# The keys' low part on all 128 rows: the second score product of the causal attentions

## The chip, the cores and the metric

The kernel runs on one core of one Trainium2 chip. The metric is the time of one execution in device microseconds (us). The times below are medians of several executions; the trace is of one further execution, taken with the hardware profiler.

## The reference, cut to what matters

The program is two transformer blocks, one after the other, on 512 tokens of width 1024. The change lies in the first block, which has two layers. Each layer has a mixer with two kinds of attention, both with heads of width 64, and then a feed-forward part:

```python
# fox: 8 heads, causal, with a forget gate
s = jnp.einsum('bhqd,bhkd->bhqk', qi, k) * scale
s = s + ci[..., :, None] - c[..., None, :]
s = jnp.where(kpos[None, :] <= qpos[:, None], s, -jnp.inf)
p = jax.nn.softmax(s, axis=-1)
o = jnp.einsum('bhqk,bhkd->bhqd', p, v)
# nsa: 8 query heads in 2 groups that share keys and values; three branches
#   compressed keys (31 blocks), selected blocks, and a window of 512
o_n = g[..., 0:1] * o_c + g[..., 1:2] * o_s + g[..., 2:3] * o_w
```

With 512 tokens there are 8 blocks to select from and up to 16 may be taken, and the window is as long as the sequence, so the kernel computes the selected and the window branch as plain causal attentions, each with its own keys and values. Counted over a layer that makes 8 causal heads in fox and 16 in nsa (8 query heads, 2 branches); over both layers 16 and 32.

## The kernel before, in words

The matrix engine (PE) reads its operands as fp32r, a shorter format than fp32. To keep precision, the kernel splits a value into a high part (rounded to fp32r) and a low part (the rest), and adds up the products. A projection (`mm3`, lines 234 to 236) takes three matmuls for each 128 input features: high by high, high by low, low by high.

For scores the split is stacked on the rows, over which PE contracts. A head has 64 features. `q_stack` (from line 569) makes a tile `Q[h]` of 128 rows for each head: the 64 rows `own` (0 to 63 for an even head, 64 to 127 for an odd one) hold the query's high part, the other 64 rows its low part. `fox` makes the keys: `KH[:, h]` holds the key's high part on both halves of the rows (ScalarE copies, lines 467 and 468), and `KL` its low part on the head's own 64 rows alone (VectorE, line 469). `causal_scores` (from line 593) then computes, for each of the four blocks of 128 queries against the n = 128, 256, 384 or 512 keys up to its end:

- line 605: all 128 rows of `Q` by all of `KH`, which gives (query high + query low) by key high;
- line 606: the own 64 rows of `Q` by the own 64 rows of the low part, which gives query high by key low;
- in fox only, line 480: a constant selector of 128 rows by `cneg`, the forget gate's term;
- line 609: an identity by the causal mask in bf16, on the last 128 columns.

All four add up in one bank of PSUM. Then VectorE takes the row maximum (line 610), ScalarE the exponential with its sum (line 612), VectorE scales the rows (line 288), PE transposes the probabilities in pieces of 128x128 (line 629), VectorE and ScalarE copy them out into tiles `PT` (lines 635 and 633; tag `PT`, 4 buffers, used in pairs, one for each of two heads), and PE multiplies them by the values (line 638).

In `nsa` the keys of a branch lie in one tile `nK` with high and low part, and the low part is already written to both halves of the rows; yet line 606 reads only the own 64 of them. `nsa` rotates keys and queries with `rope_in` (from line 558): a shuffle (line 564), a multiply on GpSimd (line 565), a multiply and an addition on VectorE (lines 566 and 567). Its two scratch tiles `rsh` and `rzc` have one buffer each.

Within a mixer the instructions are written down in program order, but a list scheduler of the framework puts them in order for each engine, by its own estimate of their times, so that the products of attention and the projections of the parts that follow (`kp`, `vp`, `qp`, `mg`, `my` in the profile) are interleaved on PE. Buffers of one tag are handed on as they come free. In the odd mixer and the expert part of the second block the order on PE is written out by hand; the change does not touch them. All engines work through their own queue in order.

Of the kernel before, what the change touches and what calls it, by code (L numbers as in the profile page):

```python
# [11 lines left out]
F32 = mybir.dt.float32  # L12
F32R = mybir.dt.float32r
# [6 lines left out]
T = 512  # L20
# [127 lines left out]
class K:  # L148
# [303 lines left out]
    def fox(self, l, at, pp, w, XH, XL, v, cneg, B, comp):  # L452
        nc, C = self.nc, self.C
        ws, parts = {}, {}

        def project(pr):
            if pr % 2 == 0:
                ws[0] = [self.wcols(w, c + 128 * pr) for c in (0, 512)]
            wq, wk = [x[:, :, (pr % 2) * 128:(pr % 2) * 128 + 128] for x in ws[0]]
            Q = self.q_stack(at, pp, wq, XH, XL, None)  # L460
            zk = self.k_proj(at, pp, wk, XH, XL)
            KH = at.tile([128, 2, T], F32R, name="KH", bufs=2)
            KL = at.tile([128, T], F32R, name="KL", bufs=2)
            for h in range(2):
                own = slice(64 * h, 64 * h + 64)
                oth = slice(64 - 64 * h, 128 - 64 * h)
                nc.scalar.copy(KH[own, h], zk[own])
                nc.scalar.copy(KH[oth, h], zk[own])
                nc.vector.tensor_sub(KL[own], zk[own], KH[own, h])
            parts[pr] = Q, KH, KL  # L470

        def attend(pr):
            Q, KH, KL = parts.pop(pr)
            o = pp.tile([128, T], F32, name="o", tag="o")
            P, cf = [], []
            for h in range(2):
                own = slice(64 * h, 64 * h + 64)
                sel = C["sel"][:, 2 * pr + h:2 * pr + h + 1].to_broadcast([128, 128])

                extra = lambda s_, n: nc.tensor.matmul(s_[:, :n], sel, cneg[:, :n], start=False, stop=False)  # L480
                P.append(self.causal_scores(at, pp, Q[h], KH[:, h], Q[h][own], KL[own], extra))
                rs = at.tile([128, 4], F32, name="rs")
                nc.vector.reciprocal(rs, P[h][1])
                cf.append(rs)
            self.causal_pv(at, pp, o, P, cf,
                           [[v[:, k, (2 * pr + h) * 64:(2 * pr + h) * 64 + 64] for k in range(4)]
                            for h in range(2)], True, True)
            if pr:
                B.renew(pr)
            self.put_split(B, pr, o)  # L490

        project(0)
        next(comp)
        project(1)
        next(comp)
        for pr in range(4):
            attend(pr)
            if pr < 2:
                project(pr + 2)
# [58 lines left out]
    def rope_in(self, at, rc, rs, z):  # L558

        nc = self.nc  # L560
        n, c = z.shape
        sh = at.tile([128, T], F32, name="rsh", tag="rsh", bufs=1)[:n, :c]
        zc = at.tile([128, T], F32, name="rzc", tag="rzc", bufs=1)[:n, :c]
        nc.vector.stream_shuffle(sh, z, [i ^ 8 if i < 16 else i for i in range(32)])
        nc.gpsimd.tensor_mul(zc, z, rc)
        nc.vector.tensor_mul(sh, sh, rs)
        nc.vector.tensor_add(z, zc, sh)
# [22 lines left out]
        self.nc.vector.tensor_mul(z, ps, self.rB)  # L590
        return z

    def causal_scores(self, at, pp, Q, KH, qh, kl, extra=None):

        nc, C = self.nc, self.C
        P = at.tile([128, 1280], F32, name="P", bufs=3)
        sums = at.tile([128, 4], F32, name="sums", bufs=4)
        mx = at.tile([128, 4], F32, name="mx", bufs=4)
        views = []
        off = 0  # L600
        for i in range(4):
            n = 128 * (i + 1)
            qs = slice(128 * i, n)
            s = pp.tile([128, T], F32, name="s", tag="s")
            nc.tensor.matmul(s[:, :n], Q[:, qs], KH[:, :n], start=True, stop=False)
            nc.tensor.matmul(s[:, :n], qh[:, qs], kl[:, :n], start=False, stop=False)
            if extra is not None:
                extra(s, n)
            nc.tensor.matmul(s[:, qs], C["identb"], C["causal"], start=False, stop=True)  # L609
            nc.vector.tensor_reduce(mx[:, i:i + 1], s[:, :n], axis=X, op=OP.max, negate=True)  # L610
            pv = P[:, off:off + n]
            nc.scalar.activation(pv, s[:, :n], AF.Exp, bias=mx[:, i:i + 1], accum_out=sums[:, i:i + 1])  # L612
            views.append(pv)
            off += n
        return views, sums
# [25 lines left out]
    def nsa(self, l, p, at, pp, w, XH, XL, gate, gcmp, B, KC, VC, fill):  # L641
        nc, tc, I, C, rB = self.nc, self.tc, self.ins, self.C, self.rB
# [31 lines left out]
        for g in range(2):  # L674
            own = slice(64 * g, 64 * g + 64)
            Q = []
# [4 lines left out]
            s = pp.tile([128, 4, 4, 32], F32, name="s", tag="s")  # L681
            mask = C["cmpmask"].rearrange("p (t n) -> p t n", t=4)[:, :, None, :].to_broadcast([128, 4, 4, 32])
            nc.tensor.matmul(s, C["identb"], mask, start=True, stop=False)
            for t in range(4):
                qs = slice(128 * t, 128 * t + 128)
# [3 lines left out]
            s16 = s.rearrange("p t h n -> p (t h) n")  # L689
            mx = at.tile([128, 16], F32, name="cmx")  # L690
            nc.vector.tensor_reduce(mx, s16, axis=X, op=OP.max)
            Pc = at.tile([128, T], F32, name="Pc", tag="KL", bufs=2).rearrange("p (a n) -> p a n", n=32)
            nc.vector.tensor_sub(Pc, s16, mx[:, :, None].to_broadcast([128, 16, 32]))
            nc.scalar.activation(Pc, Pc, AF.Exp)
            cs = at.tile([128, 16], F32, name="cs")
# [19 lines left out]
            for s_ in range(2):  # L715
                kk = at.tile([128, 2, T], F32R, name="nK", tag="KH", bufs=2)
                kh, kl = kk[:, 0], kk[:, 1]
                for half in range(2):
                    o_ = slice(64 * half, 64 * half + 64)
                    nc.scalar.copy(kh[o_], zs[s_][own])  # L720
                for half in range(2):
                    o_ = slice(64 * half, 64 * half + 64)
                    nc.vector.tensor_sub(kl[o_], zs[s_][own], kh[own])
                for pr in range(2):
                    P, cf = [], []
                    for h in range(2):
                        hs = slice(64 * h, 64 * h + 64)
                        P.append(self.causal_scores(at, pp, Q[2 * pr + h], kh, Q[2 * pr + h][hs], kl[hs]))
                        rs = at.tile([128, 4], F32, name="rs")
                        nc.vector.reciprocal(rs, P[h][1])  # L730
                        hd = 4 * g + 2 * pr + h
                        nc.vector.tensor_mul(rs, rs, gate[:, :, 3 * hd + 1 + s_])
                        cf.append(rs)
                    self.causal_pv(at, pp, os_[pr], P, cf,
                                   [[vv[s_][:, k, 64 * g:64 * g + 64] for k in range(4)] for _ in range(2)],
                                   False, s_ == 1)
                    next(fill)
                    if pr:
                        next(fill)
# [4 lines left out]
    def compress(self, l, p, at, pp, w, XH, XL, B, mixed):  # L744
# [77 lines left out]
        KH = p.tile([128, 2, 32], F32R, name="KCH")  # L822
        KL = p.tile([128, 2, 32], F32R, name="KCL")
        zc3 = zc.rearrange("p (g n) -> p g n", g=2)
# [1222 lines left out]
```

## Time and profile before

| | |
|---|---|
| time, median of 3 runs | 3457.11 us (3451.3 to 3459.18) |
| profiled execution: its own time, its span | 3446.95 us, 3445.2 us |
| PE matmuls | busy 3255.6 us (94%), 14746 instructions |
| PE weight loads | busy 2111.6 us (61%) |
| VectorE (DVE) | busy 1553.8 us (45%) |
| ScalarE (ACT) | busy 1051.8 us (31%) |
| GpSimd (POOL) | busy 581.3 us (17%) |
| mean granted clock of PE | 0.978 |

The span runs from the first to the last instruction of the profiled execution. A busy share is an average over stages with different limits; matmuls are pipelined, so the durations of neighbours overlap, and what a matmul costs is read from one start to the next.

### The profile page before, as it was taken

To read this page: it belongs to the slowest core of one execution; us is meant where nothing else is said; L and a number is where in the kernel's file an instruction comes from. 1 tells how busy PE (TensorE), PEld (TensorE's weight loads), DVE (VectorE), ACT (ScalarE), POOL (GpSimd) and SP (SyncE) were. 2 spreads that over 40 slices of the span, in tenths; PEclk is the share of its full clock that TensorE was granted. 3 is DMA by queue.
4 is the path that set the end of the run, shared out by engine and by line. 5 is a ranking of instruction groups with operands and counts; after the bars stand their busy time and mean duration, and the time that the engine had idled before them with its cause. 6 is when DMAs were issued, how large, how long until landed. Compare 5 with 4: busy or idle time off the path is not lost. (4 is left out here: it accounts for less than half of the span.)

```text
span 3445.2 us, 37016 instructions
## 1 busy us (share of the span) xinstructions
PE 3255.6 (94%) x14746; PEld 2111.6 (61%) x14746; DVE 1553.8 (45%) x2435; ACT 1051.8 (31%) x1856; POOL 581.3 (17%) x437
## 2 busy tenths in 40 slices
PE   8999999999999999999998889999998889999997
PEld 5666678888766666888875676434345547444343
DVE  6555464334655545444458755122124666211214
ACT  3333333223344333322246423111113443111011
POOL 2012121001101111200121224000002552200001
PEclk9999999999999999999999989999999999999998
DMA  5101132224310111233321115999994113999997
GB/s 186 50 25 50 49 99 86 94 92 136 98 49 25 49 49 63 96 98 98 98 71 39 50 60 205 421 421 396 420 421 178 37 38 122 372 421 395 421 421 296
DMA packets 223724, 585.07 MB, mean 170 GB/s; under 512 B 17600, under 2 KB 160320, under 8 KB 173376
## 3 DMA queue, kind: packets, MB, share of 16 engines
q1 hardware_dynamic: 223120, 581.92, 44.6%
q8 instruction: 116, 1.90, 0.2%
q10 hardware_dynamic: 432, 0.79, 0.1%
q14 instruction: 56, 0.46, 0.0%
HBM read 580.57 MB, written 2.10 MB: 169 GB/s over the span
## 5 line engine op out<-in xcount | busy, mean ns | idle before, releaser
L225 ACT CAST whi<-w 128x1024 fp32r<-128x1024 f32 (+1 forms) x312 | 311.1, 1003 | 709.7 <-PE mm L235 501.6
L1725 PE MATMUL a<-w,xg 128*64 128x512 f32 x2048 | 477.6, 596 | 50.4 <-DMA w<-in_w_dram 50.4
L234 PE MATMUL mm<-h,whi 128*128 128x512 f32 x1056 | 416.3, 394 | 4.8 <-ACT whi L225 4.1
L236 PE MATMUL mm<-h,wlo 128*128 128x512 f32 x1056 | 414.3, 393 | 0.4 <-POOL wlo L228 0.3
L235 PE MATMUL mm<-l,whi 128*128 128x512 f32 x1056 | 412.2, 391 | 0.0
L228 DVE TENSOR_TENSOR wlo<-w,whi 128x1024 fp32r<-128x1024 f32 (+1 forms) x235 | 301.6, 1286 | 213.5 <-ACT whi L225 212.8
L1725 PEld LDWEIGHTS a<-w,xg 128*64 128x64 f32 x2048 | 155.1, 137 | 356.2 <-issue 249.5
L228 POOL TENSOR_TENSOR wlo<-w,whi 128x1024 fp32r<-128x1024 f32 x77 | 171.8, 2235 | 565.2 <-ACT whi L225 541.0
L234 PEld LDWEIGHTS mm<-h,whi 128*128 128x128 f32 x1056 | 198.7, 188 | 48.8 <-ACT whi L225 5.3
L236 PEld LDWEIGHTS mm<-h,wlo 128*128 128x128 f32 x1056 | 198.7, 188 | 45.7 <-DVE wlo L228 0.8
L235 PEld LDWEIGHTS mm<-l,whi 128*128 128x128 f32 x1056 | 198.7, 188 | 44.8 <-issue 0.7
L1725 PE MATMUL y<-w,hT 128*64 128x512 f32 x1024 | 224.7, 594 | 0.0
L1818 DVE SCALAR_TENSOR_TENSOR th<-th,a 128x512 f32<-128x512 f32 x32 | 22.0, 687 | 327.6 <-ACT th L1817 327.6
L610 DVE TENSOR_REDUCE mx<-s 128x1 f32<-128x128 f32 x192 | 93.4, 489 | 153.6 <-PE s L609 152.8
L1725 PEld LDWEIGHTS y<-w,hT 128*64 128x64 f32 x1024 | 72.0, 137 | 140.2 <-issue 138.1
L956 POOL TENSOR_TENSOR u<-u 128x512 f32<-128x512 f32 x64 | 66.6, 1040 | 521.4 <-ACT E L955 275.5
L612 ACT ACTIVATE P<-s,mx 128x128 f32<-128x128 f32 x192 | 101.1, 528 | 166.3 <-DVE mx L610 153.7
L1793 POOL TENSOR_TENSOR og<-OH,aff 128x512 f32<-128x512 f32 x16 | 16.8, 1048 | 716.5 <-DVE oT L1836 700.0
L1817 ACT ACTIVATE th<-a 128x512 f32<-128x512 f32 x32 | 19.1, 597 | 341.6 <-PE a L1725 341.6
L1857 DVE SCALAR_TENSOR_TENSOR yl<-y,gate,yh 128x512 fp32r<-128x512 f32 x32 | 24.0, 751 | 208.9 <-ACT yh L1856 208.9
L967 DVE TENSOR_TENSOR y<-mm,r 128x512 f32<-128x512 f32 x64 | 44.2, 691 | 160.7 <-PE mm L236 160.7
L629 PEld LDWEIGHTS pt<-c_ident,P 128*128 128x128 f32 x480 | 54.4, 143 | 76.1 <-issue 64.8
(614 smaller groups left out, 6326.5 us busy)
## 6 DMA issues: line engine op xcount, KB each, us to landing
w<-in_w_dram SPq DMA_DIRECT2D x384, 1024.0 KB, 12.9
w<-in_w_in_dram SPq DMA_DIRECT2D x32, 1024.0 KB, 5.2
w<-in_w_up_dram SPq DMA_DIRECT2D x32, 1024.0 KB, 5.4
w<-in_w_down_dram SPq DMA_DIRECT2D x32, 1024.0 KB, 5.1
w<-in_w_out_dram SPq DMA_DIRECT2D x8, 1024.0 KB, 5.1
w<-in_w_o_dram SPq DMA_DIRECT2D x8, 1024.0 KB, 4.7
w<-in_ple_gate_w_dram SPq DMA_DIRECT2D x16, 512.0 KB, 9.4
w<-in_w_in_even_dram SPq DMA_DIRECT2D x7, 1024.0 KB, 5.6
```

Of the source, the lines that this page charges most:

```text
L225: nc.scalar.copy(h, view)
L228: e.tensor_sub(l, view, h)
L234: mm(ps, wh, xh, start=first, stop=False)
L235: mm(ps, wh, xl, start=False, stop=False)
L236: mm(ps, wl, xh, start=False, stop=last)
L610: nc.vector.tensor_reduce(mx[:, i:i + 1], s[:, :n], axis=X, op=OP.max, negate=True)
L612: nc.scalar.activation(pv, s[:, :n], AF.Exp, bias=mx[:, i:i + 1], accum_out=sums[:, i:i + 1])
L629: nc.tensor.transpose(ps[:, (i - k) * 128:(i - k + 1) * 128], P[h][0][i][:, k * 128:(k + 1) * 128], C["ident"])
L956: nc.gpsimd.tensor_mul(u, u, u)
L967: nc.vector.tensor_mul(y, ps, r2)
L1725: nc.tensor.matmul(ps[64 * a:64 * a + 64], lhs(a, 4 * kc + k), cw[a][:, k], start=kc == 0 and k == 0, stop=kc == 1 and k == 3)
L1857: nc.vector.scalar_tensor_tensor(yl, y, gate, yh, op0=OP.mult, op1=OP.subtract)
```

## The change

The low part of the keys in fox becomes as wide as the high part, and line 606 takes all 128 rows in both attentions, with the same weights `Q[:, qs]` as line 605. So the product of the query's low part and the key's low part is now added as well. The two scratch tiles of `rope_in` give up their own buffers and take theirs from the four of the tag `PT`, so that the memory of the pool stays the same. The compressed probabilities `Pc`, which share the tag of `KL`, are given the new size of that tag and use half of it.

```diff
-            KL = at.tile([128, T], F32R, name="KL", bufs=2)
+            KL = at.tile([128, 2, T], F32R, name="KL", bufs=2)
             for h in range(2):
                 own = slice(64 * h, 64 * h + 64)
                 oth = slice(64 - 64 * h, 128 - 64 * h)
                 nc.scalar.copy(KH[own, h], zk[own])
                 nc.scalar.copy(KH[oth, h], zk[own])
-                nc.vector.tensor_sub(KL[own], zk[own], KH[own, h])
+                for o_ in (own, oth):
+                    nc.vector.tensor_sub(KL[o_, h], zk[own], KH[own, h])
...
-                P.append(self.causal_scores(at, pp, Q[h], KH[:, h], Q[h][own], KL[own], extra))
+                P.append(self.causal_scores(at, pp, Q[h], KH[:, h], KL[:, h], extra))
...
-        sh = at.tile([128, T], F32, name="rsh", tag="rsh", bufs=1)[:n, :c]
-        zc = at.tile([128, T], F32, name="rzc", tag="rzc", bufs=1)[:n, :c]
+        sh = at.tile([128, T], F32, name="rsh", tag="PT", bufs=4)[:n, :c]
+        zc = at.tile([128, T], F32, name="rzc", tag="PT", bufs=4)[:n, :c]
...
-    def causal_scores(self, at, pp, Q, KH, qh, kl, extra=None):
+    def causal_scores(self, at, pp, Q, KH, KL, extra=None):
...
             nc.tensor.matmul(s[:, :n], Q[:, qs], KH[:, :n], start=True, stop=False)
-            nc.tensor.matmul(s[:, :n], qh[:, qs], kl[:, :n], start=False, stop=False)
+            nc.tensor.matmul(s[:, :n], Q[:, qs], KL[:, :n], start=False, stop=False)
...
-            Pc = at.tile([128, T], F32, name="Pc", tag="KL", bufs=2).rearrange("p (a n) -> p a n", n=32)
+            Pc = at.tile([128, 2, T], F32, name="Pc", tag="KL", bufs=2)[:, 0].rearrange("p (a n) -> p a n", n=32)
...
-                        P.append(self.causal_scores(at, pp, Q[2 * pr + h], kh, Q[2 * pr + h][hs], kl[hs]))
+                        P.append(self.causal_scores(at, pp, Q[2 * pr + h], kh, kl))
```

## Rows read from the trace of the kernel before

**Rows 1.** Busy us by stretch: PE, PEld, DVE, ACT, POOL; granted clock, DMA share, GB/s.

```profile
88.00:215.00 127.00, 125.80 (x524) 81.33 (x522) 76.22 (x154) 51.40 (x116) 10.29 (x7) 0.96 0.14 42
215.00:431.00 216.00, 216.00 (x978) 135.63 (x977) 106.55 (x240) 83.19 (x205) 38.55 (x20) 0.99 0.14 44
957.00:1083.00 126.00, 124.64 (x526) 80.56 (x524) 76.03 (x154) 51.43 (x116) 10.28 (x7) 0.97 0.14 42
1083.00:1306.00 223.00, 221.22 (x981) 137.44 (x980) 110.89 (x242) 84.11 (x208) 38.94 (x20) 0.98 0.14 43
```

**Rows 2.** Longest waits of PE's matmuls, 80 to 420 and 960 to 1310 us: total, times, longest.

```profile
PE vcp L835 <- DVE mixed L833: 0.9, 1, 0.9
...
PE o L638 <- DVE PT L635: 1.3, 1, 1.3
```

**Rows 3.** Line 606's matmuls: duration ns min/median/max, first and last start us, forms.

```profile
L606 PE MATMUL s<-nK,Q x128: 322/434/517, 215.4 to 1304.9; 64*128 64x128 f32 x32, 64*128 64x256 f32 x32, 64*128 64x384 f32 x32, 64*128 64x512 f32 x32
...
L606 PE MATMUL s<-KL,Q x64: 322/408/792, 88.2 to 1074.3; 64*128 64x128 f32 x16, 64*128 64x256 f32 x16, 64*128 64x384 f32 x16, 64*128 64x512 f32 x16
```

**Rows 4.** Timeline of PE in nsa: start us, us, engine, line, tiles, weights, moving operand.

```profile
308.94 0.48 PE L235 MATMUL my<-l,whi 128*128 128x512 f32 x1
309.26 0.39 PE L236 MATMUL my<-h,wlo 128*128 128x512 f32 x1
...
310.88 0.39 PE L234 MATMUL my<-h,whi 128*128 128x512 f32 x1
311.11 0.39 PE L605 MATMUL s<-nK,Q 128*128 128x512 f32 x1
311.43 0.50 PE L606 MATMUL s<-nK,Q 64*128 64x512 f32 x1
311.86 0.23 PE L609 MATMUL s<-c_causal,identb 128*128 128x128 bf16 x1
```

**Rows 5.** Timeline of PE in fox, n = 128 and 256, then 512.

```profile
104.13 0.33 PE L606 MATMUL s<-KL,Q 64*128 64x128 f32 x1
104.38 0.33 PE L480 MATMUL s<-cneg,c_sel 128*128 128x128 f32 x1
...
104.88 0.38 PE L606 MATMUL s<-KL,Q 64*128 64x256 f32 x1
105.19 0.38 PE L480 MATMUL s<-cneg,c_sel 128*128 128x256 f32 x1
...
141.82 0.48 PE L605 MATMUL s<-KH,Q 128*128 128x512 f32 x1
142.23 0.49 PE L606 MATMUL s<-KL,Q 64*128 64x512 f32 x1
142.65 0.50 PE L480 MATMUL s<-cneg,c_sel 128*128 128x512 f32 x1
142.99 0.23 PE L609 MATMUL s<-c_causal,identb 128*128 128x128 bf16 x1
```

**Rows 6.** Timeline of PE's weight loads, in brackets the idle time before one.

```profile
310.88 0.19 PEld L605 LDWEIGHTS s<-nK,Q 128*128 128x128 f32 x1
311.43 0.18 PEld L606 LDWEIGHTS s<-nK,Q 64*128 64x128 f32 x1 [0.35 <-issue]
```

**Rows 7.** Timeline of PE in nsa, products with the compressed keys (32 columns).

```profile
217.03 0.26 PE L688 MATMUL s<-KCL,Q 128*128 128x32 f32 x1
217.14 0.26 PE L687 MATMUL s<-KCH,Q 128*128 128x32 f32 x1
```

**Rows 8.** Line 469, the keys' low part in fox; columns as in Rows 3.

```profile
L469 DVE TENSOR_TENSOR KL<-zk,KH x16: 671/683/699, 71.8 to 1012.4; 64x512 fp32r<-64x512 f32 x16
```

**Rows 9.** Timeline of one rotation: GpSimd's multiply and VectorE's last addition.

```profile
149.61 2.16 POOL L565 TENSOR_TENSOR rzc<-h,c_rc 128x512 f32<-128x512 f32 x1 [57.68 <-issue]
...
153.39 0.69 DVE L567 TENSOR_TENSOR h<-rzc,rsh 128x512 f32<-128x512 f32 x1
```

More of the change, by code (lines that the diff above doesn't have):

```diff
@@ L476, in attend @@
             for h in range(2):
-                own = slice(64 * h, 64 * h + 64)
                 sel = C["sel"][:, 2 * pr + h:2 * pr + h + 1].to_broadcast([128, 128])
                 extra = lambda s_, n: nc.tensor.matmul(s_[:, :n], sel, cneg[:, :n], start=False, stop=False)
-                P.append(self.causal_scores(at, pp, Q[h], KH[:, h], Q[h][own], KL[own], extra))
+                P.append(self.causal_scores(at, pp, Q[h], KH[:, h], KL[:, h], extra))
                 rs = at.tile([128, 4], F32, name="rs")
@@ L726, in nsa @@
                     for h in range(2):
-                        hs = slice(64 * h, 64 * h + 64)
-                        P.append(self.causal_scores(at, pp, Q[2 * pr + h], kh, Q[2 * pr + h][hs], kl[hs]))
+                        P.append(self.causal_scores(at, pp, Q[2 * pr + h], kh, kl))
                         rs = at.tile([128, 4], F32, name="rs")
```

## The prediction

> **What bounds the kernel now.** I read the busy shares by stage first, then what the matrix engine (PE) waits for there, then the matmuls one by one.
>
> The two products that the change touches run in two stretches, one for each layer of the first block, and each stretch has a part for the forget-gate attention ("fox") and a part for the block-sparse one ("nsa"). By the busy time of each stretch [rows 1], PE is busy 125.8 of 127, 216 of 216, 124.6 of 126 and 221.2 of 223 us; VectorE has 76.2, 106.6, 76.0 and 110.9, so 60% at most, and ScalarE less. The granted clock is 0.96 to 0.99, nearly all of it the 2.4 GHz level. Such a busy share can hide idle time, since matmuls overlap and their ends are modelled, so I look at the waits: in 340 and 350 us the longest that PE's matmuls waited for another engine is 0.9 and 1.3 us [rows 2]. PE's own stream sets the pace of both stretches. Whatever shortens it moves everything behind it forward, as the stages that follow take the mixer's result.
>
> Second, that stream itself. A product of 128 queries with n keys is three matmuls (four in fox): line 605 contracts 128 rows (query high and low part against the key's high part), line 606 only 64 rows (query high, key low), then, in fox, line 480 (128 rows, the forget gate), and last line 609 (128 rows, bf16, the causal mask). There are 128 of line 606 in nsa and 64 in fox, in equal numbers of n = 128, 256, 384 and 512 [rows 3]: 32 and 16 attention heads of four. I read the step from one start to the next, as the durations overlap. Behind a plain projection matmul the next one starts after 0.23 us at n = 512 (310.88 to 311.11). From line 605 to 606 it takes 0.32 (311.11 to 311.43), and from 606 to 609 0.43 [rows 4]. The weight loads say why [rows 6]: the load for line 605 starts at 310.88, while the matmul ahead of it streams, 0.23 us before its own matmul; the load for line 606 starts at 311.43, together with its own matmul, after a gap of 0.35 us. Weights of 64 rows are not loaded behind a matmul of 128 rows, and on the way back the next load is late as well.
>
> **The change part by part.**
>
> *Entering line 606.* With 128 rows in line 606 the step into it becomes that of two full products of one type. At n = 512: 0.32 becomes 0.23 behind a projection, saving 0.09 [rows 4]. Behind a bf16 mask, line 605 shows 0.41 (141.82 to 142.23) [rows 5] where a projection matmul in the same place shows 0.32 (308.94 to 309.26) [rows 4]: again 0.09. I take it for 256, 384 and 512. At n = 128 a full load sets a floor: 32-column products with 128-row weights follow each other by 0.11 us [rows 7]; the saving lies between 0 and 0.09, and I take 0.04. A head: 0.04 + 3 x 0.09 = 0.31 us.
>
> *Leaving it in nsa.* The bf16 mask follows at 0.43; behind the 128-row line 480 it follows at 0.34 (142.65 to 142.99) [rows 5], 0.09 less, and I take this for all four sizes: 0.36 a head.
>
> *Leaving it in fox.* Line 480 is full rows of the same type, so here the whole step shrinks to the plain one. Now it is 0.25, 0.31 and 0.42 at n = 128, 256 and 512 [rows 5], some 0.055 for each 128 columns, so 0.365 at 384. The plain step is 0.23 at 512; less 0.055 each, that is about 0.175 and 0.12, with the floor of 0.11 below: 0.14 + 0.19 + 0.19 + 0.19 = 0.71 a head.
>
> *Sum on PE.* nsa 32 x (0.31 + 0.36) = 21.4 us; fox 16 x (0.31 + 0.71) = 16.3 us; together 37.7 us. Bounds: with nothing saved at n = 128 on entering, 48 x 0.04 = 1.9 less; with 0.09 there, 2.4 more.
>
> The Trainium skill, page "TensorE: Matmul & The Clock Gate", Part 3, "What overlaps and what doesn't", speaks against the change: a weight load overlaps matmuls in flight only when its row group differs. By that rule a 128-row load behind a 128-row matmul would be as exposed as the 64-row load now, the steps would stay, and the sum on PE would be 0. The trace disagrees: the load at 310.88 runs under a full-row matmul [rows 6].
>
> *VectorE.* The low part is now also written to the other 64 rows: one more subtraction for each of the 16 in fox, 0.683 us each [rows 8], 10.9 us in all. In nsa both halves were written already. What covers them: keys are projected ahead; the first low part is made at 71.8 us [rows 8] and first used by a product at 88.2 [rows 3], and VectorE has 40% of the stretch free [rows 1]. Queued behind them are maxima of scores and copies of transposed probabilities, for which PE would wait if they were late. I take 0; with the cover gone, 10.9.
>
> *The rotary scratch.* The two scratch tiles leave their own single buffers and share the four of the transposed probabilities. That frees successive rotations from each other, but a rotation holds two of the four: from GpSimd's multiply at 149.61 until VectorE's last addition ends at 154.08, 4.5 us [rows 9]. There are 12 large ones (six a layer: two keys, four queries). Meanwhile the transposed copies of one key block have only two buffers, and the next block's copies must wait for PE to use them. GpSimd's queue and VectorE's matter here, since the scratch is held until both have come to it. PE has projections to run meanwhile, interleaved by the scheduler. Bounds 0 and 12 x 4.5 = 54; the waits for such copies were 1.3 us at longest [rows 2], so I take 2.
>
> *What PE waits for next.* Maximum, exponential, scaling, transpose and copy take as long as before while PE comes sooner, above all at the end of nsa where no projections are left. I take 4 us, of bounds 0 and 15 (40% of the gain). Instructions may be ordered anew around all this; that is within the same bounds. The scores' other operands, the loads from memory and the compressed probabilities, which share the tag of the keys' low part, keep their buffer counts.
>
> Sum: -37.7 + 0 + 2 + 4 = -31.7 us. On the profiled execution's own 3446.95 us this gives 3415; the runs shown have their median at 3457.11, 10 us higher, and there it gives 3425, which I state.
>
> **The rivals.**
>
> *Half of it is given back*: PE meets the chain of maximum, exponential and copy, or the new order is worse: savings of 8 to 22 us, 3435 to 3449. For: in-order queues with no idle time on PE are hard to keep. Against: VectorE and ScalarE are far from full [rows 1].
>
> *64 rows cost no more than 128*: the exposed time belongs to the alternation with other products or to the load itself, and remains. Then PE gains nothing and the 10.9 us on VectorE are hidden: 3457, or up to 3468 with the cover gone. The rule above would have this outcome. Against: full-row neighbours with the same types show the shorter steps [rows 4, 5].
>
> *The shared buffers stop PE (slower)*: each of the 12 rotations keeps probabilities from being copied, and PE, which takes its instructions in order, stands at the product that needs them. At the full 4.5 us each it costs 54, so 54 - 38 = 16 slower: 3473. It decides from 38 / 12 = 3.2 us a rotation. Against: two buffers are enough for one key block, and projections lie between.
>
> **How the numbers follow.** The full effect, 22 to 42 us: 0.73. Half given back: 0.16. No gain from rows: 0.05. Shared buffers stop PE: 0.06. A difference under 0.2% (7 us) cannot be told from none here. Faster than that: 0.73 and nearly all of 0.16, so 0.88; slower: most of 0.06 and a little of the 0.05 with the cover gone, 0.06; within: 0.06. The range runs from the upper bound of the gain, 42 us, plus the 6 to 8 us by which the runs shown differ (3407), to a gain of some 10 us (3447), which takes in most of the second case and leaves out about 0.15.
>
> **What would show it.** In the changed profile: the weight load of line 606 ahead of its matmul instead of beside it; steps of 0.23 from 605 to 606 behind a projection and 0.34 from 606 to the mask at n = 512; in fox 0.23 from 606 to 480; PE still over 98% busy in both stretches, each 14 to 19 us shorter; 32 subtractions into the low part instead of 16, none named as what PE waits for. Wrong would be: the load still beside its matmul (64 rows were not the cause); waits of PE for the copies of probabilities near the rotations (shared buffers); long waits for the exponential in the last 30 us of nsa (the chain).

## The result, and the profile after

The changed kernel takes 3422.93 us (median of 4 runs, 3419.62 to 3427.73) beside 3454.6 us for the kernel before (4 runs): a ratio of 0.9908, interval 0.989 to 0.9927, so 31.7 us less. The prediction was 3425 us, 31.7 us below its own base. Measured once more, beside 17 runs of the kernel before: 3423.91 us, ratio 0.9910 (0.9898 to 0.9922).

The time agrees; what it is made of does not. First the stretches of [rows 1] in the changed kernel. They are cut as there: fox and what follows it up to nsa's first score product, then nsa up to its last score product.

```profile
88.00:217.00 129.00, 121.09 (x565) 82.03 (x563) 77.05 (x158) 53.91 (x121) 8.38 (x6) 0.97 0.14 42
217.00:421.00 204.00, 198.89 (x938) 133.64 (x937) 108.63 (x243) 80.67 (x200) 40.44 (x21) 0.95 0.15 47
948.00:1075.00 127.00, 119.34 (x562) 81.12 (x561) 76.97 (x158) 53.51 (x121) 8.40 (x6) 0.99 0.14 42
1075.00:1275.00 200.00, 194.63 (x940) 131.00 (x939) 108.94 (x243) 80.50 (x200) 40.45 (x21) 0.97 0.16 48
```

Nsa has become shorter, by 12 and 23 us, but the two stretches with fox have not: 129 and 127 us, where [rows 1] has 127 and 126. Fox's own score products are done 12 us sooner in each layer. What has grown is the piece between fox's last score product and nsa's first, here in the first layer, before and then changed:

```profile
206.47 0.50 PE L606 MATMUL s<-KL,Q 64*128 64x512 f32 x1
215.20 0.31 PE L605 MATMUL s<-nK,Q 128*128 128x128 f32 x1
...
195.27 0.40 PE L606 MATMUL s<-KL,Q 128*128 128x512 f32 x1
216.80 0.31 PE L605 MATMUL s<-nK,Q 128*128 128x128 f32 x1
```

That piece took 8.7 us and now takes 21.5, in both layers: 25.6 us more in all. Over the four stretches PE is idle for 26.0 us, the length less PE's busy time, where it was idle for 4.3. The longest of PE's waits in the second layer (columns as in [rows 2]):

```profile
PE s L605 <- ACT P L612: 3.9, 5, 1.4
PE s L687 <- DVE Q L583: 3.5, 1, 3.5
```

The second stands at the border from fox to nsa: the first product with the compressed keys waits for a query. The first is the chain of maximum and exponential, which has to let go of a score bank before line 605 can write it.

The steps of PE, first nsa and then fox at n = 512, answer to [rows 4, 5]:

```profile
277.39 0.39 PE L236 MATMUL my<-h,wlo 128*128 128x512 f32 x1
277.62 0.40 PE L605 MATMUL s<-nK,Q 128*128 128x512 f32 x1
277.86 0.40 PE L606 MATMUL s<-nK,Q 128*128 128x512 f32 x1
278.10 0.23 PE L609 MATMUL s<-c_causal,identb 128*128 128x128 bf16 x1
...
138.46 0.47 PE L605 MATMUL s<-KH,Q 128*128 128x512 f32 x1
138.78 0.40 PE L606 MATMUL s<-KL,Q 128*128 128x512 f32 x1
139.01 0.40 PE L480 MATMUL s<-cneg,c_sel 128*128 128x512 f32 x1
139.25 0.23 PE L609 MATMUL s<-c_causal,identb 128*128 128x128 bf16 x1
```

Entering line 606 takes 0.24 us behind a projection (0.32 before) and 0.32 behind the mask (0.41). Leaving it to the mask in nsa takes 0.24, not the 0.34 that I had set. In fox, leaving it to line 480 takes 0.23 as set, and the step from line 480 to the mask has shrunk too, from 0.34 to 0.24. The load of line 606 now runs ahead of its matmul, under the one before it (compare [rows 6]), and so does that of line 480. The last line is line 480's load in the kernel before, which had started with its own matmul at 142.65:

```profile
277.40 0.19 PEld L605 LDWEIGHTS s<-nK,Q 128*128 128x128 f32 x1
277.63 0.19 PEld L606 LDWEIGHTS s<-nK,Q 128*128 128x128 f32 x1
278.09 0.10 PEld L609 LDWEIGHTS <-identb 128*128 128x128 bf16 x1 [0.28 <-issue]
...
138.78 0.19 PEld L480 LDWEIGHTS s<-cneg,c_sel 128*128 128x128 f32 x1
...
142.65 0.18 PEld L480 LDWEIGHTS s<-cneg,c_sel 128*128 128x128 f32 x1 [0.24 <-issue]
```

So each product saves 0.10 us more than I had counted: 192 x 0.10 = 19 us on top of 37.7, some 57 us. (At n = 128 half of that 0.10 lies in entering line 606, which saves 0.09 there too: from 0.15, 151.56 to 151.71, to 0.06, 147.02 to 147.08.) That 31.7 arrived means that some 25 us were given back, as much as the piece between fox and nsa has grown. VectorE's timeline shows a candidate, the first rotation of a key in the changed kernel:

```profile
203.74 0.29 DVE L635 COPY PT<-pt 128x128 f32<-128x128 f32 x1 [1.57 <-PE pt L629]
203.96 0.72 DVE L564 STREAM_SHUFFLE rsh<-h 128x512 f32<-128x512 f32 x1
```

GpSimd had begun its multiply for this rotation at 149.61 in the kernel before [rows 9]; now its first step comes at 203.96, 0.2 us after the start of VectorE's last copy of fox's probabilities.

### The profile page after: what moved, and what is told of

Its sections match the earlier page's. It is cut to its first block, busy times and chain, and to the rows that moved or that the text cites. A ratio compares the mean times of both kernels' runs of the same rounds, so it can differ in the third digit from the quotient of the medians.

```text
span 3422.0 us, 37023 instructions
## 1 busy us (share of the span) xinstructions
PE 3207.0 (94%) x14746; PEld 2109.4 (62%) x14746; DVE 1559.6 (46%) x2451; ACT 1051.4 (31%) x1856; POOL 581.4 (17%) x437
## 5 line engine op out<-in xcount | busy, mean ns | idle before, releaser
L234 PE MATMUL mm<-E,whi 128*128 128x512 f32 x256 | 99.7, 389 | 0.0
```

Of the source, the lines that this page charges most:

```text
L234: mm(ps, wh, xh, start=first, stop=False)
```

## The experiments

Theory A: the shared scratch costs the 25 us, because the rotations have to stand behind fox's probabilities. Theory B: PE, once faster, is stopped by the chain of maximum, exponential and copy, whatever the scratch does.

**The shared scratch alone.**

```diff
-        sh = at.tile([128, T], F32, name="rsh", tag="rsh", bufs=1)[:n, :c]
-        zc = at.tile([128, T], F32, name="rzc", tag="rzc", bufs=1)[:n, :c]
+        sh = at.tile([128, T], F32, name="rsh", tag="PT", bufs=4)[:n, :c]
+        zc = at.tile([128, T], F32, name="rzc", tag="PT", bufs=4)[:n, :c]
```

> The kernel before, with only the two scratch tiles of the rotation moved into the four buffers of the transposed probabilities. Theory A, the shared buffers give back some 20 us of the gain because a rotation may not start before the fox attention's last copies have let go of their buffers: key rotations move from 149.6 us to about 204 us, PE waits some 3 to 4 us in each layer at the first product with the compressed keys, and the kernel is 8 to 24 us slower than before. Theory B, PE simply outruns maximum, exponential and copy once its products are shorter, and the sharing is harmless: within 4 us of before.

Measured: 3481.32 us, ratio 1.0077 (1.0057 to 1.0097): 25.4 us slower, a little past the end of what theory A gave, and B is out as the account of these 25 us. Its stretches, cut at the same products as in [rows 1], and its first rotation:

```profile
91.00:237.00 146.00, 137.40 (x574) 88.55 (x572) 78.09 (x156) 55.62 (x123) 12.18 (x8) 0.95 0.15 44
237.00:447.00 210.00, 207.33 (x928) 132.09 (x926) 112.56 (x237) 79.42 (x198) 36.48 (x19) 0.97 0.13 41
973.00:1118.00 145.00, 136.65 (x573) 87.72 (x572) 77.74 (x156) 55.09 (x122) 12.25 (x8) 0.95 0.15 44
1118.00:1331.00 213.00, 209.43 (x929) 132.73 (x927) 106.47 (x238) 79.45 (x198) 35.98 (x19) 0.96 0.13 40
```

```profile
217.56 0.29 DVE L635 COPY PT<-pt 128x128 f32<-128x128 f32 x1 [1.57 <-PE pt L629]
217.77 0.72 DVE L564 STREAM_SHUFFLE rsh<-h 128x512 f32<-128x512 f32 x1
```

Again 0.2 us behind the start of VectorE's last copy of fox's probabilities. The four stretches are 714 us long instead of 692, and again it is the piece between fox's last score product and nsa's first that has grown, from 8.7 us to 28.3 and 27.8, while nsa itself is 6 and 10 us shorter. PE is idle for 23.2 us in the four where it was idle for 4.3, and their granted clock is 0.95 to 0.97 instead of 0.96 to 0.99, so a little more of them passes at the 1.2 GHz level. The wait that I had expected at the compressed keys lies elsewhere in this kernel (4.7 us, at a projection); that part of the expectation missed.

**The rows alone, with the scratch still shared.** The changed kernel with line 606 back on its own rows:

```diff
-            nc.tensor.matmul(s[:, :n], Q[:, qs], KL[:, :n], start=False, stop=False)
+            nc.tensor.matmul(s[:, :n], qh[:, qs], kl[:, :n], start=False, stop=False)
```

> The changed kernel with line 606 put back to the own 64 rows; the wide low part with its second subtractions and the shared scratch stay. This leaves the rows alone as the difference to the changed kernel. Both theories: the exposed weight load returns, steps of 0.43 us from line 606 to the mask at n = 512. By the steps read from the two traces (1.08 us for each of 32 heads in nsa and 1.46 us for each of 16 in fox) the rows are worth 58 us on PE. Theory A: slower than before by 8 to 24 us, as the shared scratch alone. Theory B: within 4 us of before, as nothing outruns the chain.

Measured: 3484.39 us, ratio 1.0084 (1.0065 to 1.0103). To the shared scratch alone that is 3 us, which its intervals don't tell from nothing: the second subtractions cost little or nothing. To the changed kernel it is 61.5 us: that is what the rows are worth here, the 57 us of the steps and a little more.

**The scratch elsewhere, same memory.** Both scratch tiles in one buffer of the low part's tag:

```diff
-        sh = at.tile([128, T], F32, name="rsh", tag="PT", bufs=4)[:n, :c]
-        zc = at.tile([128, T], F32, name="rzc", tag="PT", bufs=4)[:n, :c]
+        if c == T:
+            both = at.tile([128, 2, T], F32, name="rsc", tag="KL", bufs=2)
+            sh, zc = both[:, 0], both[:, 1]
...
```

(The small rotation of the compressed keys keeps the shared tag, in a branch that is left out here.)

> The changed kernel with the rotation's scratch moved from the buffers of the probabilities to the two of the keys' low part, which nsa otherwise uses only for its compressed probabilities; the memory stays the same. Theory A: key rotations start before 175 us again, the 3.6 us waits at the first product with the compressed keys go, and the kernel is 12 to 25 us faster than the changed one, 3398 to 3411 us beside 3423. Theory B: within 5 us of the changed kernel.

Measured: 3405.34 us, ratio 0.9857 (0.9835 to 0.9878): 17.6 us faster than the changed kernel, inside theory A's range. The first rotation's shuffle begins at 171.1 us, 33 us sooner than in the changed kernel.

**128 rows in nsa alone,** scratch as before:

```diff
-                        P.append(self.causal_scores(at, pp, Q[2 * pr + h], kh, Q[2 * pr + h][hs], kl[hs]))
+                        P.append(self.causal_scores(at, pp, Q[2 * pr + h], kh, Q[2 * pr + h], kl))
```

> The kernel before with 128 rows in line 606 of nsa alone, where the low part already lies on both halves; fox and the scratch as before. PE's steps shrink by 32 heads x 1.08 = 34.5 us. Theory A: nearly all of it arrives, 26 to 34 us faster than before, since the scratch has its own buffers. Theory B: the chain of maximum, exponential and copy takes back about half, 12 to 22 us faster.

Measured: 3436.13 us (3419.05 to 3440.84), ratio 0.9932 (0.9908 to 0.9956): 19.8 us, in theory B's range by its median. The times alone do not decide: its runs spread by 22 us with the mean granted clock, from 3419.05 at 0.978 to 3440.84 at 0.971, and runs of the kernel before do the same (3446.84 at 0.978, 3462.72 at 0.972). At equal clock the difference is 25 to 32 us (3437.56 beside 3462.72 at 0.972, 3423.55 beside 3455.91 at 0.975). The trace decides for the stretches. These are the two of nsa in the run of 3419.05 us, from first to last score product:

```profile
214.00:413.00 199.00, 198.86 (x973) 132.51 (x974) 105.47 (x239) 82.71 (x205) 38.66 (x20) 0.99 0.16 48
1065.00:1270.00 205.00, 203.21 (x983) 133.60 (x982) 110.08 (x241) 84.10 (x208) 39.04 (x20) 0.99 0.15 47
```

They were 216 and 223 us long. From the start of the first product to that of the last it is 199.4 and 204.4 us instead of 215.6 and 221.9, 34 us less where the steps promise 34.5, and PE is idle for 2 us. So here the chain takes back nothing to speak of, as theory A has it. Why four of the six runs were granted a lower clock stays open.

**Rows and scratch apart.** The variant with the scratch in the low part's buffers, with 64 rows in both attentions, and with 128 in fox alone:

> As the variant with the rotation's scratch in the buffers of the keys' low part, but with line 606 on the own 64 rows in both attentions; the wide low part and its second subtractions stay. The difference to that variant is the rows alone, without the shared buffers of the probabilities. Theory A (the scratch was what gave time back): the steps' 58 us arrive nearly whole, so this kernel stands 48 to 58 us above that variant, 3453 to 3463, and within 8 us of before. Theory B (shorter products meet the chain of maximum, exponential and copy): the difference is under 40 us.

Measured: 3454.73 us, ratio 0.9990 (0.998 to 0.9999). That scratch costs nothing, and the rows are worth 49.4 us by the medians, or (0.9990 - 0.9857) x 3456 = 46 by the ratios, each to its own runs of the kernel before: just inside or just below theory A's range, and above B's. This trace also names what the first rotation waits for. The product is the last of fox's third pair of heads that reads that pair's low part (line 606 is 610 here):

```profile
177.09 0.50 PE L610 MATMUL s<-KL,Q 64*128 64x512 f32 x1
177.73 1.29 POOL L569 TENSOR_TENSOR rsc<-h,c_rc 128x512 f32<-128x512 f32 x1 [86.13 <-PE s L610]
```

That is the order of the program: pairs one to four of fox take the tag's two buffers in turn, and the first rotation takes the one that pair three gives up. In both layers of all three variants with the scratch in this tag, GpSimd's multiply starts 0.53 to 0.64 us after the start of that product.

> The same with 128 rows in fox alone and 64 in nsa. The steps of fox are worth 16 heads x 1.46 = 23 us. Theory A: 18 to 25 us below the variant with 64 rows in both. Theory B: under 15 us.

Measured: 3438.58 us, ratio 0.9941 (0.9927 to 0.9956): 16 to 17 us below the 64 rows, between the two theories. Nsa brings the rest, 29 to 33 of its 34.5 us. Some 10 of the 57 us are not seen in this pair. About 4 of them are a wait that both variants with 128 rows in fox show in each layer, and the one with 64 rows does not: the next query projection waits for VectorE to take the one before it out of its bank.

```profile
PE qp L234 <- DVE zq L579: 1.9, 1, 1.9
```

By which wait or order the rest is lost stays open.

**What exposes the load.** Line 605 on the own 64 rows too:

```diff
-            nc.tensor.matmul(s[:, :n], Q[:, qs], KH[:, :n], start=True, stop=False)
+            nc.tensor.matmul(s[:, :n], qh[:, qs], KH[own, :n], start=True, stop=False)
```

> The kernel before with line 605 on the own 64 rows as well, the same rows and weights as line 606; this leaves out the query's low part by the key's high part. It measures what exposes the load of 64-row weights. Theory S, the change between 64 and 128 rows: the step from 605 to 606 at n = 512 is 0.23 us, and the late load moves to line 605, whose step from a projection becomes 0.32; the time stays within 8 us of before. Theory G, by the rule of the Trainium skill (TensorE: Matmul & The Clock Gate, Part 3) that a load overlaps matmuls in flight only when its row group differs: here it is the same, the step is 0.40 to 0.43, and the kernel is 18 to 36 us slower.

Measured: 3462.63 us in one run, beside a median of 3458.35 for the kernel before. The steps, then the loads:

```profile
254.08 0.39 PE L234 MATMUL my<-h,whi 128*128 128x512 f32 x1
254.40 0.49 PE L605 MATMUL s<-nK,Q 64*128 64x512 f32 x1
254.73 0.39 PE L606 MATMUL s<-nK,Q 64*128 64x512 f32 x1
255.06 0.23 PE L609 MATMUL s<-c_causal,identb 128*128 128x128 bf16 x1
```

```profile
254.40 0.18 PEld L605 LDWEIGHTS s<-nK,Q 64*128 64x128 f32 x1 [0.36 <-issue]
254.50 0.19 PEld L606 LDWEIGHTS s<-nK,Q 64*128 64x128 f32 x1
255.05 0.10 PEld L609 LDWEIGHTS <-identb 128*128 128x128 bf16 x1 [0.36 <-issue]
```

The second load of 64 rows, in the same row group, starts at 254.50, under the matmul of line 605 and 0.23 us before its own: theory G is out, by the load and by the time of this one run. (The two products have the same weights here; 64 rows of other weights were not tried.) Late is the load at the change from 128 to 64 rows, that of line 605. The mask's load, at the change back, is late too, but that alone says nothing: with 128 rows all the way it is late as well (278.09 in the changed kernel), where only the type changes, from fp32r to bf16. What speaks for the way back is the step into the mask, 0.33 here and 0.24 there, and in fox line 480's load, late behind 64 rows (142.65) and early behind 128 (138.78). Theory S holds for the loads and the time, but not for its 0.23: the step from 605 to 606 is 0.33, because a late load is booked to the matmul that it belongs to (line 605 "starts" with its load at 254.40). The same booking is in the numbers of before: the step out of the first matmul behind a change carries about 0.1 of it. The late loads are in keeping with the Trainium skill, page "TensorEngine Tiling (Array Packing)", section "Key Properties": changing the tiling mode, not just the tile, drains the engine.

**Keys or queries.** On the kernel before, the shared scratch for the two key rotations of a layer alone, then for the four query rotations alone (`shared` is a new argument of `rope_in`, true for the rotations named):

```diff
-        sh = at.tile([128, T], F32, name="rsh", tag="rsh", bufs=1)[:n, :c]
-        zc = at.tile([128, T], F32, name="rzc", tag="rzc", bufs=1)[:n, :c]
+        buf = lambda k: dict(tag="PT", bufs=4) if shared else dict(tag=k, bufs=1)
+        sh = at.tile([128, T], F32, name="rsh", **buf("rsh"))[:n, :c]
+        zc = at.tile([128, T], F32, name="rzc", **buf("rzc"))[:n, :c]
```

> The kernel before, with the scratch of the keys' two rotations of each layer in the buffers of the probabilities; the queries' rotations keep their own. By the trace of the kernel with all of it shared, the wait lies at the end of fox, where the first rotations stand behind fox's last probabilities. Theory K, it is the keys that cost: their rotations begin only after 200 us and hold up the queries' products with them; 10 to 20 us slower than before. Theory Q, the queries cost: within 6 us of before.

Measured: 3460.71 us, ratio 1.0020 (1.0012 to 1.0029): 5.5 us.

> The kernel before, with the scratch of the queries' four rotations of each layer in the buffers of the probabilities; the keys' rotations keep their own. Theory Q: with the rotation late, the queries' scratch holds up the next query projection, which PE could have run between fox's products, and in the second half of nsa the first query waits for the first group's last probabilities: 10 to 20 us slower than before, and the two parts add up to the 25 us of all of it. Theory K: within 6 us of before.

Measured: 3471.5 us, ratio 1.0050 (1.0037 to 1.0063): 16.3 us. The queries carry most, as theory Q has it, and the two add up to 21.8 of the 25.4 us. Their first rotation, too, comes 0.2 us after the start of VectorE's last copy of fox:

```profile
217.64 0.29 DVE L636 COPY PT<-pt 128x128 f32<-128x128 f32 x1 [1.57 <-PE pt L630]
217.86 0.73 DVE L565 STREAM_SHUFFLE rsh<-zq 128x512 f32<-128x512 f32 x1
```

That the late query holds up the next query projection, whose result needs the single buffer of `zq`, is argued from the code and was not tried by itself.

> The changed kernel once more, on the same chip as the two parts: 28 to 36 us faster than before, by either theory, to set beside the variant with one scratch tile of its own (58 us faster).

Measured: the 3423.91 us given above, 31 us faster than the runs of the kernel before beside it.

**One scratch tile with a buffer of its own.** GpSimd multiplies in place, so that one scratch tile with a buffer of its own is enough, and the low part lies in three half tiles, so that it fits:

```diff
-            KL = at.tile([128, 2, T], F32R, name="KL", bufs=2)
+            KL = [at.tile([128, T], F32R, name="KL", bufs=3) for _ in range(2)]
...
-        sh = at.tile([128, T], F32, name="rsh", tag="PT", bufs=4)[:n, :c]
-        zc = at.tile([128, T], F32, name="rzc", tag="PT", bufs=4)[:n, :c]
+        sh = at.tile([128, T], F32, name="rsh", bufs=1)[:n, :c]
...
-        nc.gpsimd.tensor_mul(zc, z, rc)
+        nc.gpsimd.tensor_mul(z, z, rc)
...
-        nc.vector.tensor_add(z, zc, sh)
+        nc.vector.tensor_add(z, z, sh)
...
```

> The changed kernel with the rotation's scratch cut to one tile with its own buffer (GpSimd multiplies in place, after the shuffle has read) and the low part in three half tiles, so that it fits. Theory A: rotations start near 150 us again and never share with the probabilities; faster than the variant with the scratch in the low part's buffers by 2 to 8 us, 3397 to 3403. Theory B: no difference to it, as PE is paced by the chain.

Measured: 3400.16 us (3397.91 to 3403.16), ratio 0.9831 (0.9815 to 0.9848): 58.2 us faster than before, as much as the steps promise. It is 5 us below the variant with the scratch in the low part's buffers by the medians and 9 by the ratios, whose intervals overlap, so these times don't separate the two. Its stretches, cut as before:

```profile
87.00:201.00 114.00, 110.28 (x531) 77.41 (x530) 79.04 (x156) 51.74 (x116) 12.93 (x8) 1.00 0.17 49
201.00:406.00 205.00, 203.68 (x975) 134.22 (x975) 107.82 (x245) 81.71 (x204) 37.04 (x19) 0.98 0.15 46
934.00:1046.00 112.00, 110.03 (x527) 76.47 (x524) 78.61 (x154) 51.03 (x115) 10.18 (x7) 1.00 0.16 48
1046.00:1248.00 202.00, 200.90 (x975) 132.83 (x975) 107.96 (x247) 82.74 (x206) 39.48 (x20) 0.98 0.15 48
```

The four are 633 us long, 59 less than before, and PE is idle for 8.1 us in them instead of the changed kernel's 26.0. The rotations have moved back (the first shuffle at 136.85 us), and the piece between fox's last score product and nsa's first is down to 3.7 us.

## Why the prediction was right, point by point

- *PE sets the pace, and shorter steps arrive.* Right: 61.5 us with the shared scratch (57 by the steps), 46 to 49 with the scratch in the low part's buffers, 58 with one tile of its own against the kernel before (in-place multiply included), and 34 of 34.5 in the nsa stretches of the variant with 128 rows in nsa alone.
- *Entering line 606.* Right at n = 512 (0.24 and 0.32 for 0.23 and 0.32). At n = 128 I took 0.04 and it saves 0.09.
- *Leaving it.* The mechanism was right, the size was off. The term "behind the 128-row line 480 it follows at 0.34" took for clean a step that itself came right behind 64 rows; the clean one is 0.24. That makes 0.10 us for each of 192 products, in nsa on the step from 606 and in fox on the step from 480 (at n = 128 half of it on entering): some 57 us where I summed 37.7.
- *VectorE's second subtractions at 0.* Right within what can be told: 3 us, with overlapping intervals, and the variant that has them with 64 rows and the scratch in the low part's buffers is no slower than before (0.9990).
- *The rotary scratch.* Wrong in size and in mechanism. I took 2 us, from bounds of 0 and 54; it measured 25.4. I had the rotations hold buffers that the probabilities need. It is the other way round: the rotations, which the scheduler had placed in the middle of fox, may not take a buffer before the last probabilities of fox have theirs, and nsa's first products, which need the rotated queries, come later behind fox. The statement ahead of the prediction that buffers of one tag are handed on as they come free was too simple for this: in the traces they go in the order of the program, behind VectorE's last copies of fox in the tag `PT` and behind the third pair of heads in the tag `KL`.
- *What PE waits for next, 4 us.* About right where the scratch is free: the fastest version gives back next to nothing. In the changed kernel the waits of line 605 for the exponential come to 3.3 and 3.9 us in the two layers, where they were 0.3 and 1.2.
- *The signs I had named.* The early load, the steps of 0.23 and the 32 subtractions came. The step of 0.34 into the mask came out at 0.24. PE was to be over 98% busy in each layer's stretches, and these 14 to 19 us shorter: it is 96% busy, and from fox's first score product to nsa's last they are 10 and 21 us shorter.

So 3425 was met by luck, through two errors of opposite sign: some 20 us too little for the rows, some 23 too little for the scratch. Of the rivals, "the shared buffers stop PE" had the right part of the change, at 25 us, but not the way in which it costs: it had PE standing at products whose probabilities could not be copied. With the rows at 57 us, 25 was too little to turn the result.

## What to carry to other kernels

A matmul of fewer rows among full-row ones pays at both changes; using all rows, even for a product that need not be there, can be cheaper, and for judging it the reference step must not itself stand next to a change. When two uses share a tag, ask which comes first in the program: the later one loses its freedom to be placed earlier, and what needs its result comes later too. And when a forecast comes true, take the change apart all the same: here one half of it was worth nearly twice the whole.

## What the runs showed of the hardware

- A late weight load is booked to its own matmul, so that part of the cost of a change of rows appears on the next step: 0.32 and 0.43 in the kernel before, 0.32, 0.33 and 0.33 with both products on 64 rows, where steps without a change take 0.23 to 0.24.
- Loads of 64 rows in one row group do overlap the matmul ahead (254.50 under the one that starts at 254.40).
- A bf16 mask behind fp32r products has a late load without any change of rows (278.09, idle for 0.28 us before it), and the step out of a projection matmul behind the mask is 0.32 instead of 0.23, in both kernels (143.03 to 143.35 before, 147.83 to 148.15 changed).
- The time of one kernel moves with the mean granted clock: runs of the kernel before go from 3446.84 us at 0.978 to 3467.54 at 0.972. The profiled execution (3446.95, at 0.978) and the median (3457.11), 10 us apart, fit this; which of the two, clock or time, follows the other was not tried.
